# Feed-forward input with even tokens in front of odd ones, and an alternating walk in the up-projections

## The chip, the cores and the metric

The kernel runs on one core of a Trainium2 chip. The metric is device microseconds of one execution; the median of several runs is compared.

The engines that appear here: TensorE (PE in the profile, its weight loads PEld) multiplies a stationary operand, loaded first, with a moving operand that streams past, and writes to PSUM. VectorE (DVE), ScalarE (ACT) and GpSimd (POOL) do the elementwise work; SyncE (SP) issues the DMAs.

## What is computed

A decoder trunk of two layers over 256 tokens of width 1024, in float32. Each layer has an attention and a feed-forward part. Only the feed-forward part matters here:

```python
def conv_ffn(h, w_up, conv_w, conv_b, w_down):
    S_ = h.shape[1]
    u = h @ w_up
    up = jnp.pad(u, ((0, 0), (CONV_W - 1, 0), (0, 0)))
    u = conv_b + sum(conv_w[j] * up[:, j:j + S_] for j in range(CONV_W))
    gate, val = jnp.split(u, 2, axis=-1)
    return (jax.nn.silu(gate) * val) @ w_down
...
x = x + conv_ffn(rmsnorm(x, ffn_norm[l]), w_up[l], conv_w[l], conv_b[l], w_down[l])
```

`h` is the RMS-normalised residual stream. `w_up` is 1024 x 5632 (twice D_FF = 2816), `w_down` 2816 x 1024. The convolution runs along the tokens, three wide, so a token needs the two before it.

## The kernel before

**Precision.** Every float32 matrix product is made of three matmuls in the type fp32r. Each operand is split into a high part (rounded to fp32r) and a low part (the rest), and high x high, high x low and low x high are added in PSUM. The weights come from HBM as units of 128 x 2048 words (1 MB), 92 in all; ScalarE makes the high part of each piece (`hi_part`, L164) and VectorE the low part (`lo_part`, L167).

**Features.** `feats` (L266 on) makes the input of a projection "by feature": it transposes the residual stream `xr[b]` (b is one of two blocks of 128 tokens) on TensorE (L271), four chunks of 128 features at a time (n is the half of the eight chunks). ScalarE multiplies by the norm's gain while it takes the result out of PSUM (`gain`, L283), and VectorE makes the high part (L286) and the low part (L287). A feature tile holds four chunks of 256 token columns. For the feed-forward, `feats` is called with `keep`: the unsplit features stay in the tiles `y` for later use. For the other projections `keep` is None. A layer calls `feats` with `keep` four times (two halves, two blocks), each with four L283, two L286 and two L287.

**Up-projection.** `ffn` (L704 on) has 22 units. Unit i holds, for each of the eight feature chunks, 128 columns of the gate and 128 of the value (j = 0 and 1). `mm` multiplies: weights are stationary, features move, 256 token columns each:

```python
nc.tensor.matmul(o, hi[:, s_], xh, start=(c == 0), stop=False)
nc.tensor.matmul(o, hi[:, s_], xl, start=False, stop=False)
nc.tensor.matmul(o, lo[:, s_], xh, start=False, stop=(c == KC - 1))
```

These are L723, L724 and L725: 22 x 2 x 8 x 3 = 1056 matmuls a layer. The first four units (`n_raw`) run on features without the RMS factor, before it is known; their result is scaled afterwards (`scale`, L752). For the rest `scale_x` multiplies `y` in place by the row factors `rb` (L736), and makes high and low parts of it again (L738, L739) in the tiles `hS`. `post` takes the three taps of the convolution from PSUM along the token columns (L756, L760, L762), the gate, and the split of the result (L771, L772).

**Other matmuls that are named later.** The query projections of the second layer (`proj`, L324 to L326) have features stationary and 256 weight columns moving. The down-projection (`Down.mm`, L628, L629, L633) has 512 weight columns moving, and the last quarter of its last block (L689 to L691) 256. All of these already walk the moving operand alternately through two halves: the weights are packed so on the host (`turned`), and the kernel has for it

```python
def turns(ap):
    return ap.rearrange("p (a t) -> p t a", a=2)

def pairs(ap):
    return ap.rearrange("p (t a) -> p t a", a=2)
```

`turns` reads column t of the first half, column t of the second, then t + 1 of each; `pairs` writes the output columns in plain order, with the shape that goes with it. The score matmuls of the attention (L494 to L496) have feature tiles stationary and walk `kd` straight.

**Order.** The order of the work is that of the program with a list of put-off steps: `tick` advances an estimated clock with each matmul, and `chain` and `require` issue the elementwise steps when they are due or needed. TensorE's stream runs through the output projection (`finish` with `by_half`: first half n = 0 of both blocks, then n = 1), the first two up units on the first four chunks, then on the last four, and then unit after unit. Weight units are fetched and split about four units ahead.

Of the kernel before, what the change touches and what calls it, by code (L numbers as in the profile page):

```python
# [10 lines left out]
AF = mybir.ActivationFunctionType  # L11
ALU = mybir.AluOpType
AX = mybir.AxisListType

P = 128
D = 1024
S = 256
NB = S // P
KC = D // P
# [41 lines left out]
def trunk(ctx: ExitStack, tc, x, xw, pos, cpk, fin, sinks, w, out):  # L61
    nc = tc.nc
# [8 lines left out]
    def nm(s):  # L71
        uid[0] += 1
        return f"{s}_{uid[0]}"
# [8 lines left out]
    def quad(dt=F32R, name="q"):  # L82
        return spaced(qd, 4 * S, dt, "q", nm(name), 15).rearrange("p (c t) -> p c t", c=4)

    def mid():
        return wk.tile([P, 512], F32, tag="m2", name=nm("m2"), bufs=6)

    def row3(n=3 * P):
        return wk.tile([P, 3 * P], F32, tag="m3", name=nm("m3"), bufs=8)[:, :n]

    def bank(tag):
        return ps.tile([P, 512], F32, tag=tag, name=nm(tag), bufs=4 if tag == "acc" else 2)

    def f(ap):
        return ap.bitcast(F32)

    def blk(b):
        return slice(b * P, (b + 1) * P)
# [4 lines left out]
# [6 lines that stand above are left out]
# [14 lines left out]
    def tick(ns):  # L123
        clock[0] += ns
        while put_off and not busy[0]:
            item = min(put_off, key=lambda t: t[0])
            if item[0] > clock[0]:
                return
            run_item(item)
# [65 lines left out]
    def used(i):  # L195

        prepare(i + 4)

    def need(i):
        require("w", i)  # L200
# [26 lines left out]
    cp = one.tile([P, NCOL], F32, name="cp")  # L227
# [10 lines left out]
    rb = one.tile([P, S], F32, name="rb")  # L238
# [10 lines left out]
    for b in range(NB):  # L249
        t = one.tile([P, NH, HD], F32, name=f"v{b}")  # L250
# [12 lines left out]
    def new_hT():  # L263

        return [(quad(), quad()) for _ in range(2)]

    def feats(b, n, sets, key, keep=None):

        ts = [bank("t"), bank("t")]
        for j in range(4):  # L270
            nc.tensor.transpose(ts[j // 2][:, (j % 2) * P:(j % 2 + 1) * P],  # L271
                                xr[b][:, (4 * n + j) * P:(4 * n + j + 1) * P], ident)
        tick(450)

        def steps(hT, g, y, m):
            c = slice(2 * m, 2 * m + 2)
            hi, lo = (part[:, c, blk(b)] for part in hT[n])
            y_ = y[:, c]

            def gain():  # L280
                for j in range(2):
                    col = g + 4 * n + 2 * m + j
                    nc.scalar.activation(y_[:, j], ts[m][:, j * P:(j + 1) * P], AF.Copy, scale=cp[:, col:col + 1])  # L283

            def parts():
                nc.vector.tensor_copy(hi, y_)  # L286
                nc.vector.tensor_tensor(out=lo, in0=y_, in1=f(hi), op=ALU.subtract)  # L287

            return gain, parts

        for k, (hT, g) in enumerate(sets):
            y = mid().rearrange("p (j t) -> p j t", j=4) if keep is None else keep[n][:, :, blk(b)]
            for m in range(2):
                gain, parts = steps(hT, g, y, m)
                chain(key, (200.0 + 1000.0 * k + 500.0 * m, gain), (500.0, parts))
# [17 lines left out]
    def hx(hT, c):  # L313
        hi, lo = hT[c // 4]
        return hi[:, c % 4], lo[:, c % 4]
# [388 lines left out]
    def ffn(layer, u_up, u_dn, hT, y, rb, after, tail=None):  # L704
        parts = []

        n_raw = 4
        hS = new_hT()

        def mm(i, up, cs_):  # L710
            need(u_up + i)
            hi, lo = wq[u_up + i]
            for j in range(2):
                o = up[j]
                for c in cs_:
                    if i < n_raw:
                        for b in range(NB):
                            require("x", b, c // 4)
                    else:
                        require("y", c // 2)  # L720
                    s_ = slice((2 * c + j) * P, (2 * c + j + 1) * P)
                    xh, xl = hx(hT if i < n_raw else hS, c)
                    nc.tensor.matmul(o, hi[:, s_], xh, start=(c == 0), stop=False)  # L723
                    nc.tensor.matmul(o, hi[:, s_], xl, start=False, stop=False)  # L724
                    nc.tensor.matmul(o, lo[:, s_], xh, start=False, stop=(c == KC - 1))  # L725
                    tick(3 * 256 / 2.4)

        def scale_x(m):

            c = slice(2 * (m % 2), 2 * (m % 2) + 2)  # L730
            y_, hi, lo = (t[:, c] for t in (y[m // 2], *hS[m // 2]))

            def times():
                for b in range(NB):
                    require("rb", b)
                nc.vector.tensor_tensor(out=y_, in0=y_, in1=rb.unsqueeze(1).to_broadcast([P, 2, S]), op=ALU.mult)  # L736

            chain(("y", m), (2000.0 + 1000.0 * m, times), (700.0, lambda: nc.scalar.activation(hi, y_, AF.Copy)),  # L738
                  (600.0, lambda: nc.vector.tensor_tensor(out=lo, in0=y_, in1=f(hi), op=ALU.subtract)))  # L739

        def post(i, up, pq):
            hi, lo = pq[:, 2 * (i % 2)], pq[:, 2 * (i % 2) + 1]
            t = [row3(S) for _ in range(2)]
            gs, h = row3(S), row3(S)
            w0, w1, w2, bb = ([cp[:, CW + (layer * 2 * NF + j * NF + i) * 4 + k:][:, :1] for j in range(2)] for k in range(4))
            us = [mid()[:, :S] for _ in range(2)] if i < n_raw else up

            def scale():
                for b in range(NB):
                    require("rb", b)  # L750
                for j in range(2):
                    nc.vector.tensor_tensor(out=us[j], in0=up[j], in1=rb, op=ALU.mult)  # L752

            def tap2():
                for j in range(2):
                    nc.scalar.activation(t[j], us[j], AF.Identity, scale=w2[j], bias=bb[j])  # L756

            def taps():
                for j in range(2):
                    nc.vector.scalar_tensor_tensor(out=t[j][:, 1:], in0=us[j][:, :S - 1], scalar=w1[j], in1=t[j][:, 1:],  # L760
                                                   op0=ALU.mult, op1=ALU.add)
                    nc.vector.scalar_tensor_tensor(out=t[j][:, 2:], in0=us[j][:, :S - 2], scalar=w0[j], in1=t[j][:, 2:],  # L762
                                                   op0=ALU.mult, op1=ALU.add)

            def gate():
                nc.scalar.activation(gs, t[0], AF.Silu)
                nc.gpsimd.tensor_tensor(out=h, in0=gs, in1=t[1], op=ALU.mult)  # L767

            steps = [(200.0, scale), (700.0, tap2)] if i < n_raw else [(200.0, tap2)]
            chain(("p", i), *steps, (400.0, taps), (1600.0, gate),  # L770
                  (3400.0, lambda: nc.scalar.activation(hi, h, AF.Copy)),  # L771
                  (450.0, lambda: nc.vector.tensor_tensor(out=lo, in0=h, in1=f(hi), op=ALU.subtract)))  # L772
            parts.append((hi, lo))

        pq = quad()
        ups = [[bank(t)[:, :S] for _ in range(2)] for t in ("u", "acc")]
        for cs_ in (range(4), range(4, KC)):
            for i in range(2):
                mm(i, ups[i], cs_)
        for i in range(2):  # L780
            used(u_up + i)
            post(i, ups[i], pq)
        for m in range(4):
            scale_x(m)
        for i in range(2, NF):
            if i % 2 == 0:
                pq = quad()
            up = bank("acc" if i < 4 else "t" if i % 2 else "u")
            mm(i, [up[:, :S], up[:, S:]], range(KC))
            used(u_up + i)  # L790
            post(i, [up[:, :S], up[:, S:]], pq)

        def wait(i):
            require("p", 2 * i)
            require("p", 2 * i + 1)

        if tail is not None:
            nc.sync.dma_start(fin_t, fin.partition_broadcast(P))
        dn = Down(u_dn, NF // 2, parts, wait, tail is not None)
        for _ in dn.units(0, NF // 2 - 2):  # L800
            pass
        dn.finish(NF // 2 - 2, after, tail)
# [20 lines left out]
    hT = new_hT()  # L823
# [186 lines left out]
    hT = new_hT()  # L1010
    y = [quad(F32, "y") for _ in range(2)]
# [28 lines left out]
    for b in range(NB):  # L1040
        o = bank("acc")
# [30 lines left out]
    hT = new_hT()  # L1072
    y = [quad(F32, "y") for _ in range(2)]
# [150 lines left out]
```

## Time and profile before

| | us |
|---|---|
| median of 3 runs | 569.88 (569.54 to 570.95) |
| the profiled execution, whole | 569.15 |
| its span, first to last instruction | 567.4 |
| mean granted clock of TensorE | 0.991 of full |
| longest waits of TensorE | 4.1 on ScalarE (L400), 2.5 on VectorE (L167), 1.3 on ScalarE (L561) |

The span is what the profile's rows add up to; 1.75 us lie around it. A row of the groups has the line, the engine, the operation, output and input by name, the sizes, the count, and then the busy time, the mean of one in ns and the idle time before. A row of the timeline has start, duration, engine, line and count. The rows of the windows have the stretch, its width, the busy time and count of each engine asked for, the granted clock, and the DMA's share and GB/s. Matmuls are pipelined: the duration of one is longer than its share of the stream, so the rate is read from the starts.

### The profile page before, as it was taken

What the parts mean: (1) busy time and instruction counts of PE and PEld (TensorE: products, weight loads), DVE (VectorE), ACT (ScalarE), POOL (GpSimd) and SP (SyncE); (2) the same over time, 40 slices, a digit from 0 to 9 for tenths busy, and PEclk for the clock granted to TensorE, in tenths of its full rate; (3) what the DMA queues carried; (4) which work ended last, traced back from release to release, by engine and by line L of the source; (5) the groups of instructions that cost most, each with busy time, mean ns of one, the idle gap of its engine ahead of it and who ended that gap; (6) DMA issues with size and microseconds to landing.
All of it is one profiled execution on the core that took longest, in us unless ns stands there. A gap on an engine that the chain in (4) does not pass through costs nothing.

```text
span 567.4 us, 10530 instructions
## 1 busy us (share of the span) xinstructions
PE 550.1 (97%) x4022; PEld 512.6 (90%) x4022; DVE 437.0 (77%) x928; ACT 379.0 (67%) x771; POOL 104.0 (18%) x130
## 2 busy tenths in 40 slices
PE   8789999999999999999999999999999999999995
PEld 7679989889999999988887988889999999998884
DVE  6589988788899888864449989878988888874414
ACT  6846887887567777753439788887666777763413
POOL 7221102002232233110000100001432233210003
PEclk9889999999999999999999999999999999999998
DMA  8834472533384666555561832333265566666301
GB/s 321 361 120 178 153 243 77 206 139 103 122 288 160 222 223 223 200 198 202 217 219 43 268 137 96 129 98 126 102 219 206 218 223 223 213 210 222 135 0 74
DMA packets 15312, 101.00 MB, mean 178 GB/s; under 512 B 1952, under 2 KB 2080, under 8 KB 3744
## 3 DMA queue, kind: packets, MB, share of 16 engines
q1 hardware_dynamic: 14976, 100.09, 49.6%
q8 instruction: 31, 0.51, 0.3%
q10 hardware_dynamic: 288, 0.26, 0.1%
q14 instruction: 17, 0.14, 0.1%
HBM read 99.30 MB, written 1.05 MB: 177 GB/s over the span
## 4 chain that ended last, share of the span: by engine, by line
PE 84%; DVE 7%; ACT 4%; DMA 2%; issue 1%; POOL 1%; SPq 0%; DVEq 0%; POOLq 0%; ACTq 0%
PE acc L628 9%; PE acc L629 9%; PE acc L633 9%; PE u L725 6%; PE u L724 6%; PE u L723 6%; PE t L725 6%; PE t L724 6%; PE t L723 6%; DVE wl L167 3%; PE acc L452 2%; PE acc L454 2%; PE acc L453 2%; PE acc L724 2%; PE acc L723 2%; PE acc L725 2%
## 5 line engine op out<-in xcount | busy, mean ns | idle before, releaser
L167 DVE TENSOR_TENSOR wl<-wr,wh 128x1024 fp32r<-128x1024 f32 (+1 forms) x208 | 222.6, 1087 | 64.8 <-ACT wh L164 63.5
L164 ACT ACTIVATE wh<-wr 128x1024 fp32r<-128x1024 f32 (+1 forms) x208 | 189.4, 944 | 63.3 <-PE acc L633 51.7
L767 POOL TENSOR_TENSOR m<-m,m 128x256 f32<-128x256 f32 x44 | 64.7, 1470 | 176.2 <-DVE m L762 111.1
L628 PE MATMUL acc<-wh,q 128*128 128x512 f32 x238 | 92.0, 386 | 0.0
L629 PE MATMUL acc<-wl,q 128*128 128x512 f32 x238 | 90.6, 380 | 0.0
L723 PE MATMUL u<-q,wh 128*128 128x256 f32 x320 | 88.4, 277 | 0.0
L724 PE MATMUL u<-q,wh 128*128 128x256 f32 x320 | 88.2, 276 | 0.0
L725 PE MATMUL u<-q,wl 128*128 128x256 f32 x320 | 88.0, 275 | 0.0
L725 PE MATMUL t<-q,wl 128*128 128x256 f32 x288 | 79.2, 275 | 0.0
L723 PE MATMUL t<-q,wh 128*128 128x256 f32 x288 | 79.2, 275 | 0.0
L724 PE MATMUL t<-q,wh 128*128 128x256 f32 x288 | 79.2, 275 | 0.0
L633 PE MATMUL acc<-wh,q 128*128 128x512 f32 x238 | 74.6, 379 | 0.0
L724 PEld LDWEIGHTS u<-q,wh 128*128 128x128 f32 x320 | 60.1, 188 | 0.0
L725 PEld LDWEIGHTS u<-q,wl 128*128 128x128 f32 x320 | 60.1, 188 | 0.0
L723 PEld LDWEIGHTS u<-q,wh 128*128 128x128 f32 x320 | 59.9, 188 | 0.0
L723 PEld LDWEIGHTS t<-q,wh 128*128 128x128 f32 x288 | 54.1, 188 | 0.0
L724 PEld LDWEIGHTS t<-q,wh 128*128 128x128 f32 x288 | 54.1, 188 | 0.0
L725 PEld LDWEIGHTS t<-q,wl 128*128 128x128 f32 x288 | 54.1, 188 | 0.0
L628 PEld LDWEIGHTS acc<-wh,q 128*128 128x128 f32 x238 | 45.0, 189 | 7.0 <-issue 0.9
L633 PEld LDWEIGHTS acc<-wh,q 128*128 128x128 f32 x238 | 45.0, 189 | 6.3
L629 PEld LDWEIGHTS acc<-wl,q 128*128 128x128 f32 x238 | 45.0, 189 | 5.9 <-issue 0.2
L771 ACT ACTIVATE q<-m 128x256 fp32r<-128x256 f32 x44 | 18.1, 416 | 40.0 <-POOL m L767 40.0
(187 smaller groups left out, 1129.4 us busy)
## 6 DMA issues: line engine op xcount, KB each, us to landing
wr<-in_w SPq DMA_DIRECT2D x90, 1024.0 KB, 4.8
first<-in_xw SPq DMA_DIRECT2D x5, 384.0 KB, 5.9
xr<-in_x SPq DMA_DIRECT2D x2, 512.0 KB, 8.2
first<-in_xw SPq DMA_DIRECT2D x1, 768.0 KB, 7.3
fin_t<-in_fin SPq DMA_DIRECT2D x1, 512.0 KB, 5.7
out<-ot SPq DMA_DIRECT2D x1, 512.0 KB, 2.6
first<-in_xw SPq DMA_DIRECT2D x1, 388.0 KB, 3.6
out<-m ACTq DMA_DIRECT2D x1, 256.0 KB, 2.1
```

Source lines behind the costliest of these rows:

```text
L164: nc.scalar.activation(wq[i][0][:, c], raws[i][:, c], AF.Copy)
L167: nc.vector.tensor_tensor(out=wq[i][1][:, c], in0=raws[i][:, c], in1=f(wq[i][0][:, c]), op=ALU.subtract)
L452: nc.tensor.matmul(om, wh, xh, start=(c == 0), stop=False)
L453: nc.tensor.matmul(om, wh, xl, start=False, stop=False)
L628: nc.tensor.matmul(pairs(o), ph[:, blk(b)], turns(hi[:, s_]), start=first, stop=False)
L629: nc.tensor.matmul(pairs(o), ph[:, blk(b)], turns(lo[:, s_]), start=False, stop=False)
L633: nc.tensor.matmul(pairs(o), pl[:, blk(b)], turns(hi[:, s_]), start=False, stop=end)
L723: nc.tensor.matmul(o, hi[:, s_], xh, start=(c == 0), stop=False)
L724: nc.tensor.matmul(o, hi[:, s_], xl, start=False, stop=False)
L725: nc.tensor.matmul(o, lo[:, s_], xh, start=False, stop=(c == KC - 1))
L767: nc.gpsimd.tensor_tensor(out=h, in0=gs, in1=t[1], op=ALU.mult)
L771: (3400.0, lambda: nc.scalar.activation(hi, h, AF.Copy)),
```

## The change

The features of the feed-forward are laid out so that, in each chunk of 256 token columns, the 128 even tokens come first and the 128 odd ones behind them. The matmuls of the up-projection read a column of the first half and one of the second in turn, and so write the tokens to PSUM in their plain order. Everything behind the up-projection is as before; the host's packing is as before.

```diff
+    def evens(ap, b):
+        return ap.rearrange("p c (a t) -> p c a t", a=2)[:, :, :, b * P // 2:(b + 1) * P // 2]
+
     def feats(b, n, sets, key, keep=None):
...
             c = slice(2 * m, 2 * m + 2)
-            hi, lo = (part[:, c, blk(b)] for part in hT[n])
-            y_ = y[:, c]
+            if keep is None:
+                hi, lo = (part[:, c, blk(b)] for part in hT[n])
+                y_ = y[:, c]
+            else:
+                hi, lo = (evens(part[:, c], b) for part in hT[n])
+                y_ = evens(y[:, c], b)
 
             def gain():
                 for j in range(2):
                     col = g + 4 * n + 2 * m + j
-                    nc.scalar.activation(y_[:, j], ts[m][:, j * P:(j + 1) * P], AF.Copy, scale=cp[:, col:col + 1])
+                    t = ts[m][:, j * P:(j + 1) * P]
+                    nc.scalar.activation(y_[:, j], t if keep is None else t.rearrange("p (t a) -> p a t", a=2), AF.Copy,
+                                         scale=cp[:, col:col + 1])
...
-            y = mid().rearrange("p (j t) -> p j t", j=4) if keep is None else keep[n][:, :, blk(b)]
+            y = mid().rearrange("p (j t) -> p j t", j=4) if keep is None else keep[n]
...
-                    xh, xl = hx(hT if i < n_raw else hS, c)
-                    nc.tensor.matmul(o, hi[:, s_], xh, start=(c == 0), stop=False)
-                    nc.tensor.matmul(o, hi[:, s_], xl, start=False, stop=False)
-                    nc.tensor.matmul(o, lo[:, s_], xh, start=False, stop=(c == KC - 1))
+                    xh, xl = (turns(t) for t in hx(hT if i < n_raw else hS, c))
+                    nc.tensor.matmul(pairs(o), hi[:, s_], xh, start=(c == 0), stop=False)
+                    nc.tensor.matmul(pairs(o), hi[:, s_], xl, start=False, stop=False)
+                    nc.tensor.matmul(pairs(o), lo[:, s_], xh, start=False, stop=(c == KC - 1))
...
-                nc.vector.tensor_tensor(out=y_, in0=y_, in1=rb.unsqueeze(1).to_broadcast([P, 2, S]), op=ALU.mult)
+                y4 = y_.rearrange("p c (a t) -> p c a t", a=2)
+                r4 = rb.rearrange("p (t a) -> p a t", a=2).unsqueeze(1).to_broadcast([P, 2, 2, P])
+                nc.vector.tensor_tensor(out=y4, in0=y4, in1=r4, op=ALU.mult)
```

In words, step by step. L283 reads a block of 128 tokens from PSUM with a step of two, first the even and then the odd ones, and writes 64 columns into each half of the chunk. L286 and L287 read and write in the same two runs of 64. L736 reads the row factors with a step of two; the features themselves it passes through in the order in which they lie. L738 and L739 are unchanged. No instruction, DMA or wait is added or taken away.

## The prediction

> **What bounds the kernel now.** I read the page from its top: the span, the busy shares, the granted clock, then the chain that ended last.
>
> ```profile
> span 567.4 us, 10530 instructions
> PE 550.1 (97%) x4022; PEld 512.6 (90%) x4022; DVE 437.0 (77%) x928; ACT 379.0 (67%) x771; POOL 104.0 (18%) x130
> PEclk9889999999999999999999999999999999999998
> PE 84%; DVE 7%; ACT 4%; DMA 2%; issue 1%; POOL 1%; SPq 0%; DVEq 0%; POOLq 0%; ACTq 0%
> ```
>
> TensorE is busy for 97% of the span and carries 84% of the chain, at nearly the full clock. The up-projections are lines 723 to 725. How many matmuls are they? The groups by shape have one row of L723 for each output tile:
>
> ```profile
> L723 PE MATMUL u<-q,wh 128*128 128x256 f32 x320 | 88.4, 277 | 0.0
> L723 PE MATMUL t<-q,wh 128*128 128x256 f32 x288 | 79.2, 275 | 0.0
> L723 PE MATMUL acc<-q,wh 128*128 128x256 f32 x96 | 25.8, 275 | 0.0
> ```
>
> 320 + 288 + 96 = 704, and L724 and L725 are issued as often: 2112 matmuls, 1056 a layer. Their 275 ns are no price, because matmuls overlap. What counts is the step from one start to the next. I take it from the windows of each layer's long undisturbed stretch (first: width, TensorE busy and count, granted clock), and from the timeline at the ends of the first:
>
> ```profile
> 131.47:243.56 112.09, 112.09 (x992) 1.00 0.55 196
> 391.44:503.54 112.10, 112.10 (x992) 1.00 0.56 200
> 131.47 0.28 PE L725 MATMUL u<-q,wl 128*128 128x256 f32 x1
> 243.56 0.28 PE L725 MATMUL t<-q,wl 128*128 128x256 f32 x1
> ```
>
> Of the 992, two had started before the window; 990 start in it, which is 989 steps: 112.09 / 989 = **113.34 ns**, in the second layer the same. TensorE is never idle there and the clock is 1.00, so this step is the limit of the stage. Whatever is taken off it comes off the end, as long as nothing else becomes late.
>
> **The change, part by part.** First the matmuls. Their moving operand (the features) is now walked alternately through two halves, 128 columns apart. The kernel already has 256-column matmuls of the same type that walk their moving operand so: the query projections, L324 to L326. Two undisturbed runs of them, windows and then the timeline at their ends:
>
> ```profile
> 328.02:330.81 2.79, 2.79 (x27) 1.00 0.14 59
> 342.24:345.37 3.13, 3.13 (x30) 1.00 0.00 0
> 328.02 0.28 PE L325 MATMUL acc<-wl,q 128*128 128x256 f32 x1
> 330.81 0.28 PE L326 MATMUL acc<-wh,q 128*128 128x256 f32 x1
> 342.24 0.28 PE L325 MATMUL acc<-wl,q 128*128 128x256 f32 x1
> 345.37 0.28 PE L326 MATMUL acc<-wh,q 128*128 128x256 f32 x1
> ```
>
> The first has 25 steps in 2.79 us (the other two of the 27 were under way when the window opened), the second 28 in 3.13: 5.92 / 53 = **111.7 ns**. Their halves lie 128 columns apart as well. So I expect 113.34 - 111.7 = 1.64 ns less for each of 2112 matmuls: **3.5 us**. With the endpoints rounded to 0.01 us the difference is good to about 0.3 ns, so 2.9 to 4.1 us.
>
> There is a rule against this. The Trainium skill, "SBUF — State Buffer", Specifications (TRN2), says that SBUF is read in 16-byte lines and that two hits in a row on a line are needed for full bandwidth. By it, a walk that jumps 512 bytes at each 4-byte word pays at every word, and the sum would turn into a loss; the rows above disagree, 111.7 ns alternating against 113.34 ns straight.
>
> Next, the preparation of the features. Instruction counts stay; only the order of words inside them changes. The groups concerned, with two by which I bound them:
>
> ```profile
> L283 ACT ACTIVATE y<-t,cp 128x128 f32<-128x128 f32 x32 | 9.4, 408 | 0.2
> L756 ACT ACTIVATE m<-u,cp 128x256 f32<-128x256 f32 x36 | 18.1, 553 | 0.0
> L286 DVE CAST q<-y 128x256 fp32r<-128x256 f32 x16 | 4.2, 285 | 0.0
> L287 DVE TENSOR_TENSOR q<-y,q 128x256 fp32r<-128x256 f32 x16 | 6.3, 416 | 0.0
> L736 DVE TENSOR_TENSOR y<-y,rb 128x512 f32<-128x512 f32 x8 | 5.5, 683 | 2.3 <-ACT rb L813 2.3
> L167 DVE TENSOR_TENSOR wl<-wr,wh 128x1024 fp32r<-128x1024 f32 x152 | 185.4, 1232 | 54.1 <-ACT wh L164 52.9 <-PE u L555 1.0
> L167 DVE TENSOR_TENSOR wl<-wr,wh 128x512 fp32r<-128x512 f32 x56 | 37.1, 695 | 10.7 <-ACT wh L164 10.7
> ```
>
> None of these orders is in the trace, so each gets two ends. L283 now reads every second word of PSUM: between its 408 ns and 553 ns, the price of L756, which reads all 256 words. L286 copies in runs of 64: between 285 and the 416 ns of L287 on the same size. L287 itself: between 416 and the 695 ns of twice the words. L736 reads every second word of the row factors: between 683 and 1232 ns, again twice the words. A gain I exclude, since the same words pass the same engine. I take the near end for L287 and L736, whose word count is unchanged, and the middle for L283 and L286.
>
> The Trainium skill, "VectorE: DVE Perf Modes", What auto-detection actually checks, says that a one-source operation within SBUF keeps its fast mode when the outer sizes are even. L286 would then stay at 285 ns, the term for it would be zero, and the sum would be some 0.1 us lower; the trace of before only shows that this copy is quicker than L287, 285 against 416 ns.
>
> What of this is on the path? Where the output projection hands over to the feed-forward, the timeline reads:
>
> ```profile
> 122.28 0.49 DVE L286 CAST q<-y 128x256 fp32r<-128x256 f32 x2
> 122.69 0.75 DVE L287 TENSOR_TENSOR q<-y,q 128x256 fp32r<-128x256 f32 x2
> 122.69 0.48 PE L723 MATMUL u<-q,wh 128*128 128x256 f32 x2
> 123.01 0.52 PE L723 MATMUL acc<-q,wh 128*128 128x256 f32 x3
> 123.36 0.28 PE L724 MATMUL u<-q,wh 128*128 128x256 f32 x1
> ```
>
> The first copy ends at about 122.57, just ahead of the first matmul at 122.69; the first low part ends at about 123.1, and L724 follows at 123.36 after five L723 that needed no low part. The cover is 0.1 to 0.3 us, so the last block before the matmuls is exposed: four L283, two L286, two L287. At my values this is 4 x 0.07 + 2 x 0.065 = 0.4 us, less the cover: I take 0.15 us a layer, **0.3 us** in all. At the far ends it is 4 x 0.145 + 2 x 0.131 + 2 x 0.279 = 1.4 us a layer, 2.8 us in all. The other half of the features is not wanted before the 48 matmuls on the first half are through, 5.4 us, and is covered by them.
>
> The scaled features come next: L736, a ScalarE copy and L739, four times, first wanted by unit 4. And VectorE has little room there (window: width, then busy and count of TensorE, weight loads, VectorE, ScalarE, GpSimd):
>
> ```profile
> 130.00:150.00 20.00, 20.00 (x178) 20.00 (x178) 18.97 (x34) 14.69 (x24) 5.04 (x3) 1.00 0.31 109
> 150.00:230.00 80.00, 80.00 (x708) 80.00 (x708) 68.15 (x110) 57.34 (x95) 23.86 (x16) 1.00 0.61 214
> 144.87 0.68 DVE L739 TENSOR_TENSOR q<-y,q 128x512 fp32r<-128x512 f32 x1
> 147.79 0.28 PE L723 MATMUL u<-q,wh 128*128 128x256 f32 x1
> 153.95 1.22 DVE L167 TENSOR_TENSOR wl<-wr,wh 128x1024 fp32r<-128x1024 f32 x1
> 158.22 0.28 PE L725 MATMUL u<-q,wl 128*128 128x256 f32 x1
> ```
>
> The last L739 ends at 145.55; unit 4 takes those two chunks up at its seventh chunk, 147.79: 2.2 us of slack. TensorE arrives 192 x 1.64 ns = 0.3 us earlier, VectorE perhaps 0.5 us later: about 1.4 us remain and the cost is zero. The weights' tightest point is unit 6, whose second low part ends at 155.17 and is used at 158.22: 3.05 us. In the steady stretch VectorE is busy 68.15 / 80 = 85%, ScalarE 72%. A stage that is 1.5% shorter raises that to 86 and 73%, so neither becomes the bound; the DMA share of 0.61 rises to 0.62. Nothing is moved past a queue, no DMA and no wait is added.
>
> Sum, against the profiled execution's 569.15 us (567.4 us of span and 1.75 around it): -3.5 + 0.3 = -3.2, so 565.95 us. The median shown, 569.88, lies 0.73 above that execution; the same saving gives **566.7 us**, 0.56% less.
>
> **The rivals.** About 0.3%, 1.7 us, is what a measurement of this kernel can tell from no change.
>
> *Not the order, but the operands (no gain).* The query projections differ in more than the walk: features are stationary there and weights move, in the up-projections it is the other way round. If that sets the 1.7 ns, the change does not do what it says and only the 0.3 us stay: 570.2 us. Against it speak the score matmuls, whose stationary operand is a feature tile too, and which walk straight:
>
> ```profile
> 324.54 0.29 PE L494 MATMUL acc<-kd,q 128*128 128x256 f32 x1
> 325.13 0.28 PE L496 MATMUL acc<-kd,q 128*128 128x256 f32 x1
> ```
>
> Six matmuls, five steps in 0.59 us: 118 ns, not 111.7. For it: no row has weights stationary and an alternating walk.
>
> *The preparation eats it (about nothing).* With the far ends, 2.8 us go at the two handovers: 569.88 - 3.5 + 2.8 = 569.2 us. If also L736 cost 1232 ns, its four delays of 0.55 us would use up the 2.2 us of slack.
>
> *The walk collides with the weight load (slower).* The 118 ns of the scores show that a 256-column step can also be longer, by tiles alone. If alternating reads of the feature tiles against loads from the weight tiles fell into such a pattern, the price would be 118 - 113.34 = 4.7 ns x 2112 = +9.8 us: 579.7 us. It decides as soon as the step exceeds 113.34 + 1.7 / 2.112 = 114.2 ns. Against it: both tiles are the kinds that L324 uses at 111.7 ns, with roles exchanged. The skill's 16-byte lines, named above, would send the step this way.
>
> *More than expected.* The tail's matmuls alternate too, and their first step is shorter:
>
> ```profile
> 559.33 0.27 PE L689 MATMUL u<-wh,q 128*128 128x256 f32 x1
> 559.44 0.28 PE L690 MATMUL u<-wl,q 128*128 128x256 f32 x1
> 560.56 0.28 PE L691 MATMUL u<-wh,q 128*128 128x256 f32 x1
> ```
>
> 0.11 us; the twelve together take 1.23 us for 11 steps, 111.8 ns, so the first can be as short as 109, my estimate within the rounding. If the up-projections kept such a step, 4.3 ns x 2112 = 9.1 us would go: 560.8 us. The later steps of that very run are back at 111.8, so this is unlikely.
>
> **How the numbers follow.** Forecast 0.74, with a range of its own from 565.8 (no handover cost, 4.1 us saved) to 568.4 (2.0 us of handover). Not the order 0.10, preparation 0.06, collision 0.05, more 0.05. The range takes in the forecast and the preparation case, 0.80 together: 565.8 to 569.8. Faster by over 0.3%: 0.74 + 0.05, less 0.01 for the forecast's own upper edge, is 0.78. Within 0.3%: 0.10 + 0.06 + 0.01, less 0.01 for mishaps beyond it, is 0.16. Slower: 0.06.
>
> **What would show it.** Right: steps of about 111.7 ns in both long stretches, each 1.6 us shorter, TensorE without idle time, and down-projections at their old pace. For the preparation: L283, L286 and L736 near 408, 285 and 683 ns, and no new gap of TensorE around 122 and 147 us. Wrong: steps still at 113.3 (the operands decide), above 114.2 (a collision), or a long stretch that starts later by more than 0.5 us (the handover).

## The result and the profile after

| | before | after |
|---|---|---|
| median, us | 570.41 (569.54 to 571.02, 4 runs) | 566.74 (565.67 to 567.12, 4 runs) |
| the profiled execution, us | 569.15 | 565.67 |
| its span, us | 567.4 | 564.0 |

The ratio of after to before is 0.9934, with a 95% interval of 0.9913 to 0.9955: 0.66% faster, and the forecast was 0.56% (3.2 us, from the 569.88 us of the three runs then known). Line numbers move in the changed kernel: the up-projections are L734 to L736, the down-projections L639, L640 and L644, the preparation L293 (was L283), L297 (L286), L298 (L287) and L749 (L736).

The page of the changed kernel, its first rows:

```profile
span 564.0 us, 10532 instructions
PE 546.4 (97%) x4022; PEld 509.1 (90%) x4022; DVE 437.9 (78%) x928; ACT 379.2 (67%) x771; POOL 108.0 (19%) x130
PE 84%; DVE 7%; ACT 4%; DMA 2%; issue 2%; POOL 1%; DVEq 0%; POOLq 0%; ACTq 0%
```

TensorE is still the bound, and it is 3.7 us less busy. The other engines do the same work: VectorE was busy for 437.0 us and is for 437.9, ScalarE 379.0 and 379.2; GpSimd's 104.0 became 108.0, and it has 1% of the chain that ended last, as before. Each engine has as many working instructions as before; the two more in the first row are semaphore instructions of TensorE's sequencer. The steps, from the windows of the two long undisturbed stretches, which begin and end with the start of a matmul:

```profile
130.63:241.85 111.22, 111.22 (x998) 1.00 0.57 199
388.83:500.05 111.22, 111.22 (x998) 1.00 0.57 204
```

Of the 998, two were under way at the window's start; 996 start in it and one more just at its end, which is 996 steps: 111.22 / 996 = **111.67 ns** in both layers, where the kernel before has 113.34.

Where did the time go? The timeline shows the first up-projection matmul and the first down-projection matmul of each layer. Before:

```profile
243.67 0.38 PE L628 MATMUL acc<-wh,q 128*128 128x512 f32 x1
...
382.67 0.38 PE L723 MATMUL u<-q,wh 128*128 128x256 f32 x1
...
503.64 0.38 PE L628 MATMUL acc<-wh,q 128*128 128x512 f32 x1
```

After:

```profile
122.81 0.47 PE L734 MATMUL u<-q,wh 128*128 128x256 f32 x2
...
241.96 0.38 PE L639 MATMUL acc<-wh,q 128*128 128x512 f32 x1
...
381.00 0.37 PE L734 MATMUL u<-q,wh 128*128 128x256 f32 x1
...
500.16 0.38 PE L639 MATMUL acc<-wh,q 128*128 128x512 f32 x1
```

The first up-projection took 243.67 - 122.69 = 120.98 us (its start stands in the prediction) and takes 241.96 - 122.81 = 119.15; the second went from 120.97 to 119.16. That is 1.8 us each, 3.6 in all. Between the two layers, from the first down-projection matmul to the next up-projection, it was 139.0 us and is 139.04. The stretches before, between and behind the two are each longer by about 0.1 us or less, 0.24 us in all, so the span is 3.4 us shorter. The whole gain lies in the matmuls that were edited, and next to none of it is given back.

### The profile page after: what moved, and what is told of

It is laid out like the page before. It is cut to its first block, busy times and chain, and to the rows that moved or that the text cites. A ratio compares the mean times of both kernels' runs of the same rounds, so it can differ in the third digit from the quotient of the medians.

```text
span 564.0 us, 10532 instructions
## 1 busy us (share of the span) xinstructions
PE 546.4 (97%) x4022; PEld 509.1 (90%) x4022; DVE 437.9 (78%) x928; ACT 379.2 (67%) x771; POOL 108.0 (19%) x130
## 4 chain that ended last, share of the span: by engine, by line
PE 84%; DVE 7%; ACT 4%; DMA 2%; issue 2%; POOL 1%; DVEq 0%; POOLq 0%; ACTq 0%
PE acc L639 9%; PE acc L640 9%; PE acc L644 9%; PE u L734 6%; PE u L735 6%; PE u L736 6%; PE t L735 6%; PE t L734 6%; PE t L736 6%; DVE wl L167 3%; PE acc L465 2%; PE acc L463 2%; PE acc L464 2%; PE acc L736 2%; PE acc L735 2%; PE acc L734 2%
## 5 line engine op out<-in xcount | busy, mean ns | idle before, releaser
L780 POOL TENSOR_TENSOR m<-m,m 128x256 f32<-128x256 f32 x44 | 68.6, 1560 | 169.2 <-DVE m L775 85.1
L639 PE MATMUL acc<-wh,q 128*128 128x512 f32 x238 | 92.0, 386 | 0.0
L640 PE MATMUL acc<-wl,q 128*128 128x512 f32 x238 | 90.6, 380 | 0.0
L734 PE MATMUL u<-q,wh 128*128 128x256 f32 x320 | 88.3, 277 | 0.0
L736 PE MATMUL u<-q,wl 128*128 128x256 f32 x320 | 87.9, 275 | 0.0
L734 PE MATMUL t<-q,wh 128*128 128x256 f32 x288 | 79.2, 275 | 0.0
L736 PE MATMUL t<-q,wl 128*128 128x256 f32 x288 | 79.2, 275 | 0.0
L644 PE MATMUL acc<-wh,q 128*128 128x512 f32 x238 | 74.6, 379 | 0.0
L736 PEld LDWEIGHTS u<-q,wl 128*128 128x128 f32 x320 | 61.4, 192 | 0.0
L735 PEld LDWEIGHTS u<-q,wh 128*128 128x128 f32 x320 | 61.4, 192 | 0.0
L734 PEld LDWEIGHTS u<-q,wh 128*128 128x128 f32 x320 | 61.3, 192 | 0.0
L734 PEld LDWEIGHTS t<-q,wh 128*128 128x128 f32 x288 | 55.3, 192 | 0.0
L735 PEld LDWEIGHTS t<-q,wh 128*128 128x128 f32 x288 | 55.3, 192 | 0.0
L736 PEld LDWEIGHTS t<-q,wl 128*128 128x128 f32 x288 | 55.3, 192 | 0.0
L639 PEld LDWEIGHTS acc<-wh,q 128*128 128x128 f32 x238 | 45.0, 189 | 7.0 <-issue 0.9
L644 PEld LDWEIGHTS acc<-wh,q 128*128 128x128 f32 x238 | 45.0, 189 | 6.3
L640 PEld LDWEIGHTS acc<-wl,q 128*128 128x128 f32 x238 | 45.0, 189 | 5.9 <-issue 0.2
```

What stands on the lines that cost most here:

```text
L639: nc.tensor.matmul(pairs(o), ph[:, blk(b)], turns(hi[:, s_]), start=first, stop=False)
L640: nc.tensor.matmul(pairs(o), ph[:, blk(b)], turns(lo[:, s_]), start=False, stop=False)
L644: nc.tensor.matmul(pairs(o), pl[:, blk(b)], turns(hi[:, s_]), start=False, stop=end)
L734: nc.tensor.matmul(pairs(o), hi[:, s_], xh, start=(c == 0), stop=False)
L735: nc.tensor.matmul(pairs(o), hi[:, s_], xl, start=False, stop=False)
L736: nc.tensor.matmul(pairs(o), lo[:, s_], xh, start=False, stop=(c == KC - 1))
```

## The experiments

Twelve kernels; times are medians where there were several runs. The steps are those of the first long stretch, worked out as above from the window quoted with each.

**The layout alone.** The changed kernel with the straight walk:

```diff
-                    xh, xl = (turns(t) for t in hx(hT if i < n_raw else hS, c))
-                    nc.tensor.matmul(pairs(o), hi[:, s_], xh, start=(c == 0), stop=False)
+                    xh, xl = hx(hT if i < n_raw else hS, c)
+                    nc.tensor.matmul(o, hi[:, s_], xh, start=(c == 0), stop=False)
...
```

> The changed kernel with the even-odd layout kept, but the up-projections walk the features straight (and so write the tokens in the permuted order: the convolution mixes the wrong tokens). Theory 'the walk': the step of the up-projection goes back from 111.7 to 113.3 ns, and the time is that of the kernel before within 0.3 us, since the preparation costs nothing: 569.9 to 570.7 us. Rival 'the layout' (the stores in two runs, or where the words lie): the step stays at 111.7 and the time at 566.7.

570.44 us, ratio to the kernel before 1.0002 (0.9992 to 1.0012). The window of its long stretch (996 steps):

```profile
131.21:244.13 112.92, 112.92 (x998) 1.00 0.55 196
```

113.4 ns. The layout by itself gains nothing and costs nothing that can be measured.

**The walk alone.** The opposite: the kernel before with `turns` and `pairs` in the three matmuls.

> The kernel before with its plain layout, but the up-projections walk the features alternately through both halves (and so write the tokens in an interleaved order: the convolution mixes the wrong tokens). Theory 'the walk': step 111.7 ns, the time is that of the changed kernel, 566.7 us, within 0.3 us; what it is shorter than that is the price of the new preparation. Rival 'the layout': 113.3 ns and 570.4 us.

566.62 us, ratio 0.9931 (0.9916 to 0.9946). Its window (997 steps), and the timeline at the ends of the first up-projection:

```profile
130.34:241.75 111.41, 111.41 (x1000) 1.00 0.55 198
122.70 0.47 PE L723 MATMUL u<-q,wh 128*128 128x256 f32 x2
241.86 0.38 PE L628 MATMUL acc<-wh,q 128*128 128x512 f32 x1
```

111.7 ns, and 241.86 - 122.70 = 119.16 us for the stage, the same as in the changed kernel. So the walk is the whole effect, and the new preparation costs nothing on the path. The rival "not the order, but the operands" has fallen: the weights stay stationary here and in the changed kernel, and only the order differs. (`turns` on the reads and `pairs` on the output go together; no run has one without the other.)

**What holds the alternating walk at 111.7 ns?** On the six middle chunks of eight, only 64 of the 128 weight columns are loaded and used, once on the changed kernel and once on the kernel before:

```diff
-                    s_ = slice((2 * c + j) * P, (2 * c + j + 1) * P)
+                    w_ = P if c in (0, KC - 1) else P // 2
+                    s_ = slice((2 * c + j) * P, (2 * c + j) * P + w_)
...
-                    nc.tensor.matmul(pairs(o), hi[:, s_], xh, start=(c == 0), stop=False)
+                    nc.tensor.matmul(pairs(o[:w_]), hi[:, s_], xh, start=(c == 0), stop=False)
```

> The changed kernel, but from the second feature chunk on only 64 of the 128 weight columns are loaded and used, except for the last matmul of a group (half of the up-projection's output features miss most of their sum). What holds the alternating walk at 111.7 ns, 5.0 above the 106.7 of 256 columns at the rate of one each 0.417 ns, which the 512-column matmuls come to within 2.5 ns (215.8)? Theory 'the load of 128 weight columns': with 64 the step falls to about 109 ns, 2112 x 2.5 = 5 us less. Rival 'the matmul by itself': it stays at 111.7.

> The same on the kernel before, with the straight walk (half of the up-projection's output features miss most of their sum). Theory 'the straight walk collides with the weight load': with half the load the 1.7 ns shrink to about 0.8 above what the alternating walk has there, so about 110 ns. Rival 'a straight walk is slower by itself': 1.7 ns above the alternating one, whatever the load; 113.3 if that stays at 111.7.

These two runs halve what is loaded, and with it what is used: half as many rows of the output are written.

Alternating: 561.80 us (one run). The timeline shows 18 matmuls in a row with 64 stationary columns, the first and the last of them:

```profile
150.79 0.27 PE L735 MATMUL t<-q,wh 128*64 128x256 f32 x1
152.64 0.27 PE L737 MATMUL t<-q,wl 128*64 128x256 f32 x1
```

17 steps in 1.85 us, about 109 ns. Straight: 569.81 us (one run), with this window (996 steps):

```profile
131.34:244.24 112.90, 112.90 (x999) 1.00 0.55 196
```

113.4 ns, as with the whole load. So the two walks answer differently. The alternating walk is held at 111.7 ns by something that goes with the 128 columns, and with 64 it goes at about 109. The straight walk stays at 113.4 with either. My theory that it collides with the weight load, at a price that shrinks with the load, has fallen. On this reading the 1.7 ns that were gained are the distance between two limits. That the first of them is the load, and not the use of the columns, is likely but not shown by these runs; a run further down changes the load alone.

**Is it that no column is followed by its neighbour?** Four other walks on the changed kernel, each with `turns` replaced by another order and the output written plainly (the tokens are then permuted):

```diff
+        return ap.rearrange("p (a t k) -> p t a k", a=2, k=2)    # runs of two
+        return ap.rearrange("p (a t k) -> p t a k", a=2, k=4)    # runs of four
+        t.rearrange("p (a t) -> p t a", a=4)                     # quarters
+        t.rearrange("p (t a) -> p a t", a=2)                     # step of two
```

> The changed kernel, but the walk takes two neighbouring columns from one half and then two from the other (the tokens are written in another order). If what matters is that no column is followed by its neighbour: back to 113.3 ns, or half way, 112.5. If what matters is that the two halves are visited within a few words: 111.7 ns as before.

> As the run with twos, but the walk takes four neighbouring columns from each half in turn (the tokens are written in another order). The twos cost 164.4 - 111.7 = 52.8 ns a matmul for 128 short runs. Theory 'a price for each short run' (about 0.41 ns each): 64 runs, 111.7 + 26 = 138 ns, total about 566.7 + 2112 x 26 ns = 622 us. Rival 'a price for the third loop of the pattern': 164 ns again, 677 us.

> The changed kernel, but the walk visits four quarters in turn, 64 columns apart, one column each (the tokens are written in another order). If it is enough that no column is followed by its neighbour: 111.7 ns, 566.7 us. If the inner loop of two is what makes it quick, or the distance of 128: a different step, 113.3 or more.

> The changed kernel, but the walk takes every second column, then the other columns (the tokens are written in another order). No column is followed by its neighbour, but by one that is 8 bytes off, mostly in the same 16 bytes. So far: halves 111.7, quarters 138.3, runs of four 131.1, runs of two 164.4, straight 113.4 ns. If not meeting the neighbour is enough: 111.7 ns. If the two far apart halves are needed: 113.4 ns or more (each group of 16 bytes is met twice, at distance).

Their windows, in this order (996 steps in the first three, 997 in the last):

```profile
133.60:297.38 163.78, 163.78 (x998) 1.00 0.38 132
```

```profile
132.59:263.17 130.58, 130.58 (x999) 1.00 0.48 169
```

```profile
131.97:269.75 137.78, 137.78 (x999) 1.00 0.45 158
```

```profile
138.41:366.11 227.70, 227.70 (x1001) 1.00 0.28 97
```

| walk | step, ns | time, us (one run) |
|---|---|---|
| two halves in turn (the change) | 111.7 | 566.74 (median) |
| straight (the layout alone) | 113.4 | 570.44 (median) |
| runs of four | 131.1 | 607.08 |
| quarters in turn | 138.3 | 621.47 |
| runs of two | 164.4 | 676.77 |
| every second column | 228.4 | 813.14 |

In the first two runs none of the values that I had written down came: 164.4 instead of 111.7 to 113.3, and 131.1 instead of 138 or 164. In the other two the first guess, that not meeting the neighbour is enough, fell, and the second, 113.3 or 113.4 "or more", held, but gave no size. So "not meeting the neighbour" is not the rule: quarters and a step of two avoid the neighbour as well and are far slower than the straight walk. A fixed price for a third loop is excluded, since runs of two and of four have the same three loops and different steps; fewer runs are cheaper, but 64 runs cost 19.4 ns over the change and 128 cost 52.8, so the price of one is not constant either. Nor is it the walk alone: 131.1 is a mean, and the three matmuls of a chunk (L741 to L743 in this kernel), which all walk by fours but read different tiles, take unequal steps, here 0.14, 0.12 and 0.13 us:

```profile
150.02 0.30 PE L741 MATMUL u<-q,wh 128*128 128x256 f32 x1
150.16 0.29 PE L742 MATMUL u<-q,wh 128*128 128x256 f32 x1
150.28 0.30 PE L743 MATMUL u<-q,wl 128*128 128x256 f32 x1
150.41 0.30 PE L741 MATMUL u<-q,wh 128*128 128x256 f32 x1
```

The Trainium skill's page "SBUF — State Buffer" (Specifications (TRN2)) asks for at least two hits on each 16-byte line for full bandwidth. The trace does not agree: the step of two meets each line twice in a row and takes twice the time of the straight walk, while the walk through two halves never does and is the fastest of all. The measurement decides. Which rule gives all six numbers stays open.

**Can PSUM take the jump, so that the layout can stay?** The kernel before; the walk by twos, and the output written in the same jumping order, so that each token keeps its place. (No run here has a jump after every single column of the output.)

> The kernel before with its plain layout; the walk takes two neighbouring columns from one half and two from the other, and the output in PSUM is written in the same jumping order, so that the result keeps its place. If the walk by twos is as good as by ones and PSUM takes a jump of 512 bytes after every two columns without a price: step 111.7 ns and 566.7 us, with no change of the layout. If a write that is not in order costs (the Trainium skill, PSUM - Partial Sum Buffer, Specifications (TRN2), has lines of 8 bytes there and says that any access that is not contiguous slows matmuls significantly): a step well above 113.3 ns, by 2112 x the difference.

677.58 us, ratio 1.1885 (1.1865 to 1.1905). Its window (996 steps):

```profile
133.96:297.75 163.79, 163.79 (x999) 1.00 0.38 132
```

164.4 ns, the same as the walk by twos with plain output. The price is that of the walk; the jumps of 512 bytes in PSUM after every two columns add nothing to it that shows. A price of their own that fits within 164.4 ns would be hidden, so whether PSUM could take the jump beside a quick read stays open. The Trainium skill's page "PSUM — Partial Sum Buffer" (Specifications (TRN2)) says that a pattern that is not contiguous slows matmuls significantly; this run neither shows that nor rules it out.

**Does the start of the tiles matter?** `SKIP` 0 instead of 4, on the kernel before and on the changed one:

```diff
-    SKIP, ROUND = 4, 64
+    SKIP, ROUND = 0, 64
```

> The kernel before, with the operand tiles starting 4 words earlier (SKIP 0 instead of 4). A straight walk is slower by itself, 113.3 ns; is that a matter of where the walk starts? The scores walk a tile straight that has no such shift, at 118 ns. Theory 'the start matters to a straight walk': the up-projections go to about 118 ns, the time to 570.2 + 2112 x 4.7 ns = 580 us or more, since lines 452 to 454 (384 matmuls) go with them. Rival 'it doesn't': 113.3 ns, 570.2 us, and the 118 of the scores has another cause.

> The same on the changed kernel. If the alternating walk is free of the start's influence as it is of the neighbours': 111.7 ns, so the distance between the two walks would be 6 ns here instead of 1.7, and the time about 567 to 569 us (lines 463 to 465 still walk straight). If the start matters to it as well: it rises by as much as the straight one.

570.86 and 566.95 us (one run each). Their windows, before and changed (997 steps each):

```profile
132.05:245.14 113.09, 113.09 (x1000) 1.00 0.56 196
```

```profile
131.74:243.16 111.42, 111.42 (x1001) 1.00 0.57 199
```

113.4 and 111.8 ns: the start does not matter to these stretches. To other matmuls that walk straight it does. The projections L452 to L454 (L463 to L465 in the changed kernel) have weights stationary and 256 feature columns moving, like the up-projections, and neither kernel lets them alternate. One of their long runs, 56 steps, in the kernel before and with `SKIP` 0 on each kernel; the line for `SKIP` 0 on the kernel before has another run of theirs, 54 steps, ahead of it:

```profile
85.25:91.59 6.34, 6.34 (x58) 1.00 0.25 105
```

```profile
50.56:56.68 6.12, 6.12 (x56) 1.00 0.81 321
86.64:93.24 6.60, 6.60 (x58) 1.00 0.25 102
```

```profile
86.42:93.02 6.60, 6.60 (x59) 1.00 0.24 101
```

113.2 ns with the shift of four words and 117.9 without it, at a granted clock of 1.00 each time; the other run keeps 113.3 without the shift. All twelve kernels here that have the shift take about 113 ns a step in the first of these runs. The kernel before shows the slower step too, with the shift, where a run of the same lines is short, just behind six transposes:

```profile
92.49 0.28 PE L453 MATMUL acc<-q,wh 128*128 128x256 f32 x1
93.31 0.28 PE L454 MATMUL acc<-q,wl 128*128 128x256 f32 x1
```

7 steps in 0.82 us, 117 ns. The straight walk has two paces in these traces, 113.3 and about 118, and 113.4 is not its pace in every place. So the 118 ns of the score matmuls, a run of six, need not come from their tile; what decides between the two paces stays open.

**Can the load be made quicker by its order?** If the load of the weights is now the limit, its order should tell: gate and value columns interleaved in HBM and loaded with a step of two.

```diff
-                    s_ = slice((2 * c + j) * P, (2 * c + j + 1) * P)
+                    s_ = slice(2 * c * P + j, 2 * (c + 1) * P, 2)
...
-            units.append(mm[:, :, :, i].transpose(1, 0, 2, 3).reshape(P, UNIT))
+            units.append(mm[:, :, :, i].transpose(1, 0, 3, 2).reshape(P, UNIT))
```

> The changed kernel, with the weight columns of gate and value interleaved in HBM, so that the stationary operand is loaded with a step of two columns (the same result). The load of 128 columns holds the step at 111.7 ns, and 64 columns at 109.1. If a load with a step is as quick: 111.7 ns, 566.7 us. If the neighbours are what slows a load, as they slow the moving operand: down to 109.1 ns, 561.3 us, faster than both kernels. If a step of 8 bytes slows it: above 111.7.

580.41 us, ratio to the kernel before 1.0195 (1.0169 to 1.022), and about 14 us more than the changed kernel. Its window (997 steps):

```profile
130.43:248.82 118.39, 118.39 (x1000) 1.00 0.53 187
```

118.7 ns, and only the order in which the stationary columns are read was changed: so the load can set the step, and a step of two makes it slower. That makes it likely, with the half loads, that the plain load is what holds 111.7 ns. The plain order of the weights stays the better of the two.

## Why the prediction was right, by its own steps

*The matmuls.* Forecast: 1.64 ns from each of 2112, 3.5 us, with the step of the query projections. Measured: 113.34 to 111.67 ns, which is 1.67 ns; the two stages together are 3.6 us shorter. What the long stretches do not account for, 3.64 us less 2112 x 1.67 ns, is 0.1 us and lies in the matmuls around them.

*Why the query projections were the right row.* Their halves lie as far apart, their matmuls have the same width and type, and they load 128 columns too. If it is this load that sets 111.7 ns, as the half loads and the interleaved load make likely, the step carried over although stationary and moving operand had changed roles. The prediction had the number without this reason.

*The preparation.* Here the groups after, by shape:

```profile
L293 ACT ACTIVATE y<-t,cp 128x128 f32<-128x128 f32 x32 | 9.4, 410 | 0.2
L297 DVE CAST q<-y 128x256 fp32r<-128x256 f32 x16 | 4.2, 286 | 0.0
L298 DVE TENSOR_TENSOR q<-y,q 128x256 fp32r<-128x256 f32 x16 | 6.3, 418 | 0.0
L749 DVE TENSOR_TENSOR y<-y,rb 128x512 f32<-128x512 f32 x8 | 5.9, 739 | 2.1 <-ACT rb L826 2.1
```

The first three are within 2 ns of before; ScalarE reads every second word of PSUM for nothing, 410 ns against 408. The Trainium skill's "VectorE: DVE Perf Modes", What auto-detection actually checks, has the copy keep its quick mode, and the trace agrees: 286 ns against 285. The term of the preparation was mis-sized: I took the middle of the bounds, 0.3 us at the handover, and it is nothing measurable. That, and the 0.1 us above, is why the gain is a little larger than forecast. L749 went from 683 to 739 ns; the forecast had taken the near end, 683, and named it among the signs, and this sign did not come. The step of two in the row factors is not enough to explain it, for the run of the layout alone has the same L749, and there it reads:

```profile
L749 DVE TENSOR_TENSOR y<-y,rb 128x512 f32<-128x512 f32 x8 | 5.5, 684 | 2.3 <-ACT rb L826 2.3
```

What made it 739 in the changed kernel stays open. It is covered:

```profile
144.53 0.67 DVE L752 TENSOR_TENSOR q<-y,q 128x512 fp32r<-128x512 f32 x1
147.49 0.28 PE L734 MATMUL u<-q,wh 128*128 128x256 f32 x1
```

The last scaled chunks are ready at 145.20 and wanted at 147.49, still 2.3 us of slack.

*The number.* That 566.7 us was met to 0.1 us is in part luck: the saving was forecast as 3.2 us and is 3.67 between the medians, and the kernel before, taken at 569.88, has a median of 570.41 with its fourth run. The two misses nearly cancel.

*The rivals.* "Not the order, but the operands" fell by the two single-part runs. The prediction's argument against it, the 118 ns of the scores, was weak: L452 to L454 show both 113.2 and 117 ns, so a short run at 118 says little about a walk. "The preparation eats it" fell by the single-part runs too. "The collision" did not come, and halving the load of the straight walk showed none either. (Its threshold is 114.1 ns and not 114.2: 113.34 + 1.7 / 2.112; nothing hangs on it.) "More than expected", 109 ns, is what the alternating walk reached with 64 columns; with 128 it did not come.

## What to carry to other kernels

Where TensorE is never idle, read the step between the starts of equal matmuls, and compare it with that of another group of the same width: 1.7 ns of difference were worth 3.6 us here. A rate carries over to an edit when what limits it is the same on both sides, so ask whether it is the moving read or the weight load. Compare long runs, since a few steps behind other work can have another pace. And a reordered walk must be measured in exactly its form: of five orders other than straight, one was quicker by 1.5% and four slower, up to double.

## What was not expected of the hardware

The order in which the moving operand is read changes the step of a 256-column fp32r matmul from 111.7 to 228.4 ns at the same count of columns. The straight order is not the quickest, and it has two paces, 113.3 and about 118 ns. Reading every second column doubles the step, although ScalarE reads every second word of PSUM for nothing (410 against 408 ns), and VectorE every second row factor (684 against 683 ns in the run of the layout alone, though 739 in the changed kernel). Loading 128 weight columns with a step of two makes the step 7.1 ns longer.
